# All groups but two of an MLP's down projection as seven block products, with their running sums in PSUM and the weight sums on GpSimd

## The chip, the cores and the metric

The kernel runs on one core of a Trainium2 chip. The metric is the device time of one execution in microseconds. Before the change the median of 3 runs was 2968.75 us (2968.43 to 2971.05).

## The reference

One layer of a streaming encoder on 512 tokens of width 2048, in float32: two groups of sequence mixers, cross-attention, an MLP and a last norm. The change lies in the MLP and the norm after it:

```python
hn = _rmsnorm(h, norm_mlp)                                # h: 512 x 2048
h  = h + jnp.square(jax.nn.relu(hn @ mlp_w_up)) @ mlp_w_down    # 2048 -> 8192 -> 2048
return _rmsnorm(h, norm_final)                            # h * rsqrt(mean(h*h) + 1e-6) * gain
```

## The kernel before

All is held transposed: channels on the 128 partitions, the 512 tokens along the free side (`HA` and `HB` are the tokens 0 to 255 and 256 to 511). The residual `h` is 16 tiles `hres[n]` of 128 x 512, which lie in pairs in eight tiles `hp`. Float32 products are made on TensorE from two parts: `split` (L127 on) casts a tile to fp32r on ScalarE (the high half, L130) and subtracts it from the tile on VectorE (the low half, L131); a product of weights and activations is then high x high, high x low and low x high. Split weights lie in the buffers `whi` and `wlo`, two of each, so the split of a product's weights begins when the product two before it is done.

**Up** (L1710 on) makes the 8192 hidden rows in 32 turns, each two rows of 128, by a scheme of seven block products instead of eight (`strassen`, L1293): the activations' and the weights' blocks are summed beforehand, seven products are made, and sums of products give the four result blocks. The weights' sums and the products' sums run on VectorE. The result, relu and square, goes to DRAM in `Ud`, one tile of 128 x 2 x 512 for each turn. The norm's factor isn't in it: the mean square of `h` is known only in the first turn (`rstd`, L1722), so `Ud` holds relu(.)^2 without the factor and its square 1 / (mean + eps) is multiplied in later: for the first eight rows in the turns 8 to 15 of up (L1726 to L1733: load, multiply, store), for the others when they are loaded for down (L1697, L1758).

**Down** (L1742 on) goes over the 8192 hidden rows in eight eighths `e`, each 8 tiles of 128 rows, and for each over four groups `g` of four result tiles `hres[4g]` to `hres[4g+3]`. Eighths 0 to 6 are the loop at L1860; the last eighth (L1929 on) is woven together with the last norm, in an order written out by hand. A group is made in one of two ways:

- full (`gemm`, L1869): for each of its four result tiles one weight block of 128 x 1024 is loaded and split, 24 matmuls of 512 columns are made, and one addition of 128 x 512 puts them into `hres[n]` (L1870).
- as a unit (`downunit`, L1780): four weight blocks a11, a12, a21, a22 are loaded (a11 and a12 into `wraw`, a21 and a22 into `wraw2`, three buffers each). VectorE makes four sums of them (L1820, `sub` at L1272), into two buffers `ws` and in place. Seven products follow, each with a split of 128 x 1024 and 24 matmuls of 256 columns into a PSUM bank of its own (tags `mm`, `mg` and `mx`, two banks each). The products' sums are made from PSUM into SBUF tiles `sl` (L1814, L1824) and into `hp` (`add`, L1810), twelve instructions.

Before the change the unit is used for groups 0 and 2 of the eighths 1 to 6, 12 groups of 28. The activations of a unit need their block differences (T1 to T4) as well: `downpair` (L1744) loads a pair of rows, multiplies them with the factor, splits them, makes four differences on VectorE and splits these. It is a generator: `aside` (L1844) hands the pairs of the next eighth to the groups, and after each product (or result tile) one step of it is issued. Before, pairs are made beside the full groups alone.

Loads of weights and of `Ud` go through SP's queue. Outside the last eighth the order on each engine follows the program text, as far as operands and buffers are ready when the program is laid out; on the chip each engine keeps its order.

## Time and profile before

| | us |
|---|---|
| median of 3 runs | 2968.75 |
| profiled execution, its span | 2967.1 |
| TensorE, busy | 2938.2 |
| VectorE, busy | 2323.9 |
| ScalarE, busy | 1520.1 |
| GpSimd, busy | 215.2 |
| up (from its second product to its last) | 624.3 |
| down: groups from the third of eighth 0 to the last eighth's start | 554.4 |
| the last eighth and the last norm | 105.9 |

In the profile PE is TensorE's matmuls, PEld its weight loads, DVE VectorE, ACT ScalarE, POOL GpSimd and SP the engine of the load queue. A row of the groups names the line, the engine, the operation, what it writes and reads (buffer numbers left out: `dr` and `dws` are weight blocks and sums of a unit, `d` its products, `dn` those of a full group, `de`, `do` a pair's rows, `dt` its differences), the shapes, the count, the busy time with the mean in ns, and the idle time before. A row of the timeline begins with the start in us and the duration in us.

### The profile page before, as it was taken

To read this page: it belongs to the slowest core of one execution; us is meant where nothing else is said; L and a number is where in the kernel's file an instruction comes from. 1 tells how busy PE (TensorE), PEld (TensorE's weight loads), DVE (VectorE), ACT (ScalarE), POOL (GpSimd) and SP (SyncE) were. 2 spreads that over 40 slices of the span, in tenths; PEclk is the share of its full clock that TensorE was granted. 3 is DMA by queue.
4 is the path that set the end of the run, shared out by engine and by line. 5 is a ranking of instruction groups with operands and counts; after the bars stand their busy time and mean duration, and the time that the engine had idled before them with its cause. 6 is when DMAs were issued, how large, how long until landed. Compare 5 with 4: busy or idle time off the path is not lost.

```text
span 2967.1 us, 51025 instructions
## 1 busy us (share of the span) xinstructions
PE 2938.2 (99%) x20106; PEld 2515.2 (85%) x20106; DVE 2323.9 (78%) x3725; ACT 1520.1 (51%) x2271; POOL 215.2 (7%) x552
## 2 busy tenths in 40 slices
PE   9999999999999999999999999999999999999998
PEld 7877887887788888889988988888888888998887
DVE  7677676676778667679748999999999688888777
ACT  6455555555556555654436555555555343343334
POOL 0212302302312000000000000000000000000000
PEclk9999999999999999999999999999999999999999
DMA  5333332333435587864323445444445334333436
GB/s 179 111 87 85 101 93 81 102 92 82 132 89 166 168 278 250 259 231 136 100 86 100 146 153 170 136 142 135 136 135 177 110 108 139 128 114 114 135 121 185
DMA packets 229312, 407.35 MB, mean 137 GB/s; under 512 B 92168, under 2 KB 115980, under 8 KB 229072
## 3 DMA queue, kind: packets, MB, share of 16 engines
q1 hardware_dynamic: 212944, 375.77, 41.0%
q10 hardware_dynamic: 16128, 28.32, 2.6%
q8 instruction: 158, 2.59, 0.4%
q14 instruction: 82, 0.67, 0.1%
HBM read 354.32 MB, written 49.69 MB: 136 GB/s over the span
## 4 chain that ended last, share of the span: by engine, by line
PE 86%; DVE 6%; DMA 4%; POOL 2%; issue 2%; ACT 1%; SPq 0%; ACTq 0%; DVEq 0%; POOLq 0%
PE up L122 21%; PE py L251 20%; PE dn L122 14%; PE op L122 5%; PE d L122 4%; PE vp L122 3%; PE at L122 3%; PE sc L122 3%; PE kp L251 3%; PE kq L251 2%; DVE wlo L131 2%; POOL sr L251 2%; DVE h L1810 1%; PE vo L122 1%; DMA wraw<-in_wqT 1%
## 5 line engine op out<-in xcount | busy, mean ns | idle before, releaser
L130 ACT CAST whi<-wraw 128x1024 fp32r<-128x1024 f32 x372 | 391.4, 1052 | 567.6 <-PE dn L122 189.9
L131 DVE TENSOR_TENSOR wlo<-wraw,whi 128x1024 fp32r<-128x1024 f32 x372 | 453.9, 1220 | 64.4 <-ACT whi L130 60.9
L122 PE MATMUL up<-cb,whi 128*128 128x512 f32 (+1 forms) x1904 | 451.4, 380 | 0.0
L251 PE MATMUL py<-xhi,whi 128*128 128x512 f32 x928 | 374.2, 403 | 6.6 <-ACT xhi L251 6.6
L122 PEld LDWEIGHTS up<-cb,whi 128*128 128x128 f32 x1904 | 330.7, 189 | 54.9 <-issue 0.2
L251 PE MATMUL py<-xlo,whi 128*128 128x512 f32 x928 | 374.2, 403 | 0.0
L251 PE MATMUL py<-xhi,wlo 128*128 128x512 f32 x928 | 373.6, 403 | 0.1
L251 ACT CAST whi<-wraw 128x1024 fp32r<-128x1024 f32 (+1 forms) x180 | 188.0, 1044 | 211.9 <-PE py L251 133.1
L251 DVE TENSOR_TENSOR wlo<-wraw,whi 128x1024 fp32r<-128x1024 f32 (+1 forms) x180 | 220.9, 1227 | 87.7 <-ACT whi L251 86.5
L122 PEld LDWEIGHTS up<-cb,wlo 128*128 128x128 f32 x1792 | 244.1, 190 | 16.4
L122 PE MATMUL up<-cb,wlo 128*128 128x256 f32 x1792 | 251.1, 282 | 0.0
L122 PE MATMUL dn<-uh,whi 128*128 128x512 f32 x640 | 244.7, 391 | 0.8 <-ACT whi L130 0.8
L122 PE MATMUL dn<-ul,whi 128*128 128x512 f32 (+1 forms) x648 | 244.7, 388 | 0.0
L122 PE MATMUL dn<-uh,wlo 128*128 128x512 f32 (+1 forms) x640 | 235.1, 367 | 0.0
L251 PEld LDWEIGHTS py<-xhi,whi 128*128 128x128 f32 x928 | 175.3, 189 | 41.6 <-ACT xhi L251 7.0
L1336 DVE TENSOR_TENSOR sl<-sl,up 128x256 f32<-128x256 f32 x464 | 182.0, 414 | 35.0 <-PE up L122 31.8
L251 PEld LDWEIGHTS py<-xlo,whi 128*128 128x128 f32 x928 | 175.2, 189 | 37.3 <-issue 3.3
L251 PEld LDWEIGHTS py<-xhi,wlo 128*128 128x128 f32 x928 | 175.2, 189 | 35.2 <-issue 1.0
L130 ACT CAST whi<-ws 128x1024 fp32r<-128x1024 f32 x120 | 126.1, 1051 | 108.7 <-PE up L122 70.4
L1972 POOL TENSOR_TENSOR h<-h,rstd 128x256 f32<-128x256 f32 x5 | 3.4, 724 | 2012.6 <-ACT rstd L1966 2012.6
L131 DVE TENSOR_TENSOR wlo<-ws,whi 128x1024 fp32r<-128x1024 f32 x120 | 146.0, 1218 | 0.5 <-ACT whi L130 0.5
L122 PEld LDWEIGHTS dn<-uh,whi 128*128 128x128 f32 x640 | 120.2, 188 | 26.5 <-ACT whi L130 1.0
(882 smaller groups left out, 6420.7 us busy)
## 6 DMA issues: line engine op xcount, KB each, us to landing
wraw<-in_w_up SPq DMA_DIRECT2D x128, 512.0 KB, 3.5
wraw<-in_w_in SPq DMA_DIRECT2D x116, 512.0 KB, 3.7
wraw<-in_w_dn SPq DMA_DIRECT2D x96, 512.0 KB, 3.5
wraw<-in_wk SPq DMA_DIRECT2D x32, 512.0 KB, 4.0
wraw<-in_wqT SPq DMA_DIRECT2D x32, 512.0 KB, 5.3
wraw<-in_wv SPq DMA_DIRECT2D x32, 512.0 KB, 4.8
wraw<-in_wo SPq DMA_DIRECT2D x32, 512.0 KB, 5.6
wraw<-in_w_out SPq DMA_DIRECT2D x32, 512.0 KB, 3.4
```

What stands on the lines that cost most here:

```text
L122: PE.matmul(o, l, r, start=start, stop=stop)
L130: S.copy(hi, src)
L131: V.tensor_tensor(out=lo, in0=src, in1=hi.bitcast(F32), op=ALU.subtract)
L251: f(*a, **k)
L1336: V.tensor_tensor(out=o, in0=a, in1=b, op=op)
L1810: V.tensor_tensor(out=h, in0=h, in1=two(src), op=ALU.add)
L1972: GP.tensor_tensor(out=h, in0=h, in1=rstd[:, HB], op=ALU.mult)
```

## The change

- Groups 2 and 3 of eighth 0 and all groups of the eighths 1 to 6 are units now, 26 of 28; only groups 0 and 1 of eighth 0 are full. `w_dm` holds the blocks of seven eighths and `w_dn` those of eighths 0 and 7 alone, laid out beforehand.
- A unit uses three banks, x, y and z. Products whose sum is needed go into the same bank one after the other: B11, T2, T3 and T4 into x, T1 and B22 into z, B21 alone into y. Between them VectorE adds what the bank holds so far to `hp`: seven additions of 128 x 512, the last of which (after T4) is issued in the next unit, behind its first product.
- The four weight sums of a unit run on GpSimd.
- A pair's differences run on GpSimd: two of 256 elements and one of 512 for two differences at once. A pair is loaded in one transfer (`uload`, tag `ab`, two buffers). Each group of eighths 1 to 5 prepares one pair of the next eighth, groups of eighth 0 two, those of eighth 6 a pair of the last eighth (`usplit`).
- The factor isn't multiplied into the hidden rows. `rstd` keeps mean + eps, and the residual is multiplied with it (eight products of 1024 elements in the turns 4 to 11 of up), so that `h` is divided by the square of the norm's factor. The last norm takes that back: it doesn't depend on such a scale except for its eps, which is put into the sum of squares (L1912 on).

The diff, its core:

```diff
-            if 3 < p < 8 and i == T1:
-                c = slice((p - 4) * P, (p - 3) * P)
-                V.reciprocal(out=rstd[:, c], in_=rstd[:, c])
-            if 7 < p < 16 and i in (B11, T3):
...
+            if 3 < p < 12 and i == T1:
+                h = hp[p - 4]
+                V.tensor_tensor(out=h, in0=h, in1=rstd.unsqueeze(1).broadcast_to([P, 2, T]), op=ALU.mult)
...
+    def uload(p):
+        cnt[0] += 1
+        ab = pu.tile([P, 1024], F32, tag="ab", name=f"ab{cnt[0]}", bufs=2)
+        nc.sync.dma_start(ab.rearrange("p (a b) -> p a b", b=T), Ud[p])
+        return ab
...
     def downpair(e, k):
+        ab = uload(4 * e + k)
...
+            t = utile(f"de{e}_{k}")
+            b[B11] = t[:, HA], t[:, HB]
+            split(ab[:, HA], *b[B11])
+        x = ab[:, HA]
+        GP.tensor_tensor(out=x, in0=ab[:, HB], in1=x, op=ALU.subtract)
         yield
...
+            oh, ol = utile(f"doh{e}_{k}"), utile(f"dol{e}_{k}")
+            split(ab[:, T:2 * T], oh, ol)
...
+        split(x, *b[T1])
+        x = ab[:, 0:T]
+        GP.tensor_tensor(out=pair2(x), in0=twice(ab[:, 3 * M:4 * M]), in1=pair2(x), op=ALU.subtract)
+        yield
+        yield
...
+        split(x, sh, sl)
+        x = ab[:, T:T + M]
+        GP.tensor_tensor(out=x, in0=x, in1=ab[:, HA], op=ALU.subtract)
+        yield
+        yield
+        split(x, *b[T4])
+        yield
...
+        def wsum(o, a, b, op=ALU.subtract):
...
+            GP.tensor_tensor(out=o, in0=a, in1=b, op=op)
+            return o
...
+        a11, a21, a22, a12 = raw(0), raw(1), raw(2), raw(3)
+        x, y, z = psb(f"dx{e}_{g}", "mx", 2), psb(f"dy{e}_{g}", "mg", 2), psb(f"dz{e}_{g}", "mm", 2)
+        s1 = wsum(None, a21, a22, ALU.add)
+        product(B11, a11, x, True)
+        s2 = wsum(None, s1, a11)
+        if held:
+            held.pop()()
+        product(B21, a12, y, True)
+        wsum(a21, a11, a21)
+        add(0, HA, x)
+        product(T2, s2, x)
+        wsum(a12, a12, s2)
+        add(0, HA, y)
+        product(T1, s1, z, True)
+        add(0, HB, x)
+        product(T3, a21, x)
+        add(1, HB, z)
+        product(B22, a12, z)
+        add(1, HB, x)
+        product(T4, a22, x)
+        add(0, HB, z)
+        held.append(lambda: add(1, HA, x))
...
-            if e and g % 2 == 0:
+            if e or g > 1:
                 downunit(e, g, beside)
```

## The prediction

> **What bounds the kernel now.** I read the page first: the busy shares, then the row of GpSimd in the 40 slices.

> ```profile
> PE 2938.2 (99%) x20106; PEld 2515.2 (85%) x20106; DVE 2323.9 (78%) x3725; ACT 1520.1 (51%) x2271; POOL 215.2 (7%) x552
> POOL 0212302302312000000000000000000000000000
> ```

> TensorE is busy 99% of the span, and GpSimd does nothing in the last two thirds, where the change puts its sums. A share of 99% says that fewer matmul columns are worth time, as long as the other engines keep up. So I cut the span into stretches: up, the 26 groups that the change touches (from the third group of eighth 0 to the start of the last eighth), one full group and one unit of them, and the last eighth.

> ```profile
> 1639.00:2263.29 624.29, 624.26 (x3668) 553.11 (x3668) 585.27 (x846) 339.37 (x521) 0.00 (x0) 1.00 0.44 146
> 2306.83:2861.22 554.39, 550.11 (x3361) 494.99 (x3360) 447.39 (x635) 208.08 (x289) 0.00 (x0) 1.00 0.36 118
> 2328.59:2350.35 21.76, 21.76 (x97) 18.02 (x96) 12.98 (x17) 7.25 (x10) 0.00 (x0) 1.00 0.29 97
> 2392.89:2413.67 20.78, 20.44 (x170) 20.24 (x169) 19.46 (x29) 10.20 (x15) 0.00 (x0) 1.00 0.28 89
> 2861.22:2967.10 105.88, 94.09 (x535) 80.71 (x533) 84.05 (x152) 52.31 (x77) 3.45 (x5) 0.96 0.58 179
> ```

> Columns: stretch, its length, then busy us (and count) of PE, PEld, DVE, ACT, POOL, the granted clock, DMA. A full group takes 21.76 us, a unit 20.78. The full group leaves VectorE a third free; in the unit VectorE is busy 19.46 of 20.78. The next rows show what a unit's products cost on TensorE, and what its last one loses.

> ```profile
> 2395.76 0.28 PE L122 MATMUL d<-uh,whi 128*128 128x256 f32 x1
> ...
> 2398.64 0.28 PE L122 MATMUL d<-dt,whi 128*128 128x256 f32 x1
> ...
> 2410.93 0.39 PE L122 MATMUL d<-dt,wlo 128*128 128x256 f32 x1 [0.34 <-DVE wlo L131]
> ```

> Two products begin 2.88 us apart, so seven need 7 x 2.88 = 20.16 us of TensorE; the rest of the 20.78 is a wait for VectorE's low half of the last weights. TensorE sets the pace, with VectorE close behind it in units.

> **The change on TensorE.** Of the 26 groups, 12 were units and 14 were full. All become units. With nothing in the way the stretch would take 26 x 20.16 = 524.2 us instead of 554.39: **30.2 us less**. That is all that can be won here.

> **What the other engines must do in a unit.** The first of a unit's four weight sums and its additions before, all on VectorE (12 units):

> ```profile
> L1820 DVE TENSOR_TENSOR dws<-dr,dr 128x1024 f32<-128x1024 f32 x12 | 14.6, 1219 | 0.9 <-DMA dr<-in_w_dm 0.9
> ...
> L1810 DVE TENSOR_TENSOR h<-h,d 128x512 f32<-128x512 f32 x72 | 48.0, 679 | 1.6 <-PE d L122 0.8
> ...
> L1810 DVE TENSOR_TENSOR h<-h,sl 128x512 f32<-128x512 f32 x36 | 23.6, 683 | 0.1
> ...
> L1814 DVE TENSOR_TENSOR sl<-sl,d 128x512 f32<-128x512 f32 x24 | 16.4, 683 | 2.3 <-PE d L122 2.3
> ```

> There were four sums of 1024 elements and 6 + 3 + 2 = 11 additions of 512. After: no sum on VectorE and 7 additions, since PSUM keeps the running sums. The price in PSUM is a wait: T2 may enter the bank of B11 only when B11's addition has read it; another product (2.88 us) lies between and the addition takes 0.68, so it costs nothing as long as VectorE isn't late. The seven low halves stay. A unit now has one pair of activations to prepare beside it in each group (before, in the full groups): three low halves of 256 elements and two of 512. Their spacing when VectorE has no gap:

> ```profile
> 2506.69 1.22 DVE L131 TENSOR_TENSOR wlo<-wraw,whi 128x1024 fp32r<-128x1024 f32 x1
> 2507.82 1.22 DVE L1272 TENSOR_TENSOR dr<-wraw,dr 128x1024 f32<-128x1024 f32 x1
> 2508.96 1.29 DVE L1758 TENSOR_TENSOR de<-de,rstd 128x512 f32<-128x512 f32 x2
> ...
> 2487.48 0.42 DVE L1272 TENSOR_TENSOR de<-do,de 128x256 f32<-128x256 f32 x1
> 2487.82 0.68 DVE L1810 TENSOR_TENSOR h<-h,sl 128x512 f32<-128x512 f32 x1
> 2488.42 1.22 DVE L131 TENSOR_TENSOR wlo<-dr,whi 128x1024 fp32r<-128x1024 f32 x1
> ```

> 1.137 us for 1024, 0.60 for 512, 0.34 for 256. So VectorE's own work in a unit is 7 x 1.137 + 7 x 0.60 + (2 x 0.60 + 3 x 0.34) = 7.96 + 4.20 + 2.22 = 14.4 us of 20.16. By itself that fits. ScalarE (10.20 us in a unit now) loses a copy and gains casts for the pair; it fits too. Loads don't grow: a group had four weight blocks of 512 KB as a full group and has four as a unit, and a pair comes in one DMA instead of two. GpSimd's queue holds nothing else here.

> **What the sums cost on GpSimd.** No row shows a sum of 1024 elements there; these are the nearest, with the VectorE instructions that ran at the same time.

> ```profile
> L1972 POOL TENSOR_TENSOR h<-h,rstd 128x256 f32<-128x256 f32 x5 | 3.4, 724 | 2012.6 <-ACT rstd L1966 2012.6
> ...
> 230.94 1.23 DVE L251 TENSOR_TENSOR wlo<-wraw,whi 128x1024 fp32r<-128x1024 f32 x1 [0.21 <-ACT whi L251]
> 231.51 1.81 POOL L251 TENSOR_TENSOR gEs<-gE,cst 128x512 f32<-128x512 f32 x1 [1.49 <-ACT gE L251]
> ...
> 673.81 1.29 POOL L251 TENSOR_TENSOR gEs<-gE,cst 128x512 f32<-128x512 f32 x1
> 674.12 2.06 DVE L251 TENSOR_TENSOR wlo<-wraw,whi 128x1024 fp32r<-128x1024 f32 x1 [0.17 <-ACT whi L251]
> ...
> 453.61 1.29 POOL L251 TENSOR_TENSOR gEs<-gE,cst 128x512 f32<-128x512 f32 x1
> 453.89 1.56 DVE L251 TENSOR_TENSOR gkn<-gk,sg 128x512 f32<-128x512 f32 x1 [0.72 <-ACT sg L251]
> ```

> And the end of the kernel, where VectorE's third input comes from PSUM and GpSimd runs the row above:

> ```profile
> 2957.64 4.01 DVE L1974 SCALAR_TENSOR_TENSOR h<-h,prm,row 128x256 f32<-128x256 f32 x10 [1.31 <-ACT rstd L1966]
> ```

> The same GpSimd product of 512 elements takes 1.29 us, and 1.81 when a low half had begun before it: it ends 233.32 - 232.17 = 1.15 us after the low half. The other way round, a low half that takes 1.23 takes 2.06 when a GpSimd product had begun: it ends 676.18 - 675.10 = 1.08 us after it. A 512 product on VectorE takes 1.56 instead of the 0.68 above, and ends 0.55 after. So while one of the two engines works on two SBUF tensors, the other waits until it is done. The last row is the exception: VectorE reads `row` from PSUM there, GpSimd runs its five `h<-h,rstd` in the same 4 us, and ten instructions in 4.01 us, 0.40 each, leave no room for a wait.

> [...]

> GpSimd's time grows by 1.29 - 0.724 = 0.57 us for 256 elements, so it holds the other off for 1.15 us with 512, about 0.58 with 256 and 1.15 + 2 x 0.57 = 2.29 with 1024 (an estimate from these rows). A unit has four sums of 1024, and its pair has two differences of 256 and one of 512: 4 x 2.29 + 2 x 0.58 + 1.15 = **11.5 us**. VectorE's own such work is 7 x 1.08 + 2 x 0.55 + 3 x 0.28 = **9.5 us** (the last by halving 0.55). Together 21.0 us in which one of the two must stand still or do something else: more than the 20.16 that TensorE needs.

> **The unit's time, from both sides.** Below: all of VectorE's 4.20 us of additions and all its waits for a cast fall where GpSimd works, and the unit takes 21.0 us. Above: each GpSimd instruction is waited out in full by a low half, and the unit takes 14.4 + 11.5 = 25.9 us. Between: additions are 4.20 of VectorE's 14.4 us, so by chance 29% of GpSimd's time falls beside one; 14.4 + 0.71 x 11.5 = 22.5 us. But VectorE can't be busy all the time:

> ```profile
> L130 ACT CAST whi<-ws 128x1024 fp32r<-128x1024 f32 x120 | 126.1, 1051 | 108.7 <-PE up L122 70.4
> ```

> That is the cast, 1.05 us; and what it waits for in the groups, in us, times and the longest:

> ```profile
> ACT whi L130 <- PE d L122: 103.1, 71, 2.4
> ```

> A cast waits until a product gives its buffer back, and the low half comes 1.05 us later. TensorE needs it two matmuls (0.24 us) into the product after next, which allows 2.88 + 0.24 - 1.05 - 1.22 = 0.85 us of delay, while a sum holds it 2.29. Behind it stand the additions for which the banks wait. Three sums also come in a row, since three buffers hold the second and third weight blocks of two units, so that the next unit's third block, which the first sum needs, is loaded only when T3's split has freed one. I take the middle of 22.5 and 25.9: **24.2 us**, that is 4.0 more than TensorE needs.

> The two units of eighth 0 have two pairs beside them: VectorE 16.6, GpSimd 13.8; from 16.6 + 0.75 x 13.8 = 26.9 to 30.4, middle 28.6 us. The four of eighth 6 have only four low halves of 256: VectorE 13.5, GpSimd 9.2; 13.5 + 0.69 x 9.2 = 19.8, so TensorE's 20.16, to 22.7; middle 21.4 us.

> Sum: 20 x 24.2 + 2 x 28.6 + 4 x 21.4 = 626.8 us, against 554.4: **72.4 us more**. Ends: 20 x 22.5 + 2 x 26.9 + 4 x 20.16 = 584.4 (+30) and 20 x 25.9 + 2 x 30.4 + 4 x 22.7 = 669.6 (+115).

> **The rest.** In up, TensorE is busy 624.26 of 624.29 us and VectorE 585.27. Eight products with the factor (1024 elements, 1.14 us each, 9.1 in all) come, and eight of 512 (0.60 each), the reciprocals and sixteen DMAs on SP's and ScalarE's queues go: some 4 us more in 39 that are free. I take nothing; its end is 4 us, if none of it finds a gap. In the last turn of up six splits instead of three follow T1: nothing, at most 3 x 0.60 = 1.8 us. In the last eighth each half gains one addition and one scaled square of 256 (about 0.8 us) on VectorE, busy 84.05 of 105.88: nothing, at most 1.6. The multiplications of the activations by the factor (0.60 each) go from the groups; that is in the sums above, since 14.4 us is without them.

> **The number.** The profiled execution spans 2967.1 us; the median of the runs is 2968.75, 1.65 above it. 2967.1 + 72.4 + 1.65 = **3041 us**, 2.4% slower.

> **Rivals.**
> Faster (chance 0.07): the sums don't hold up the low halves, so the place is the pair of engines in each unit, and the price is the 30.2 us: 2938.5 us. It decides at 554.4 / 26 = 21.3 us per unit: as long as a unit loses less than 21.3 - 20.16 = 1.1 us to GpSimd's work, the change wins. For it: the largest GpSimd instruction that the trace shows has 512 elements, in another stage. Against it: the stretched instruction is the very `wlo<-wraw,whi` that a unit makes seven times, and it was stretched by all that was left of GpSimd's work.
> No change (0.05): the order of work happens to put additions and casts beside GpSimd so well that only the 21.0 us count: 20 x 21.0 + 2 x 25.2 + 4 x 20.16 = 551.0, 3 us less, 2965 us. Against it: GpSimd's instructions wait for loads and for each other, not for VectorE's free time.
> Worse than forecast (a part of slower): each sum is waited out, 3083 us.

> **How the numbers follow.** Slower holds 0.88: 0.62 around 3041 with ends 2999 and 3070, 0.20 near full waiting up to 3085, 0.03 between no change and 2990, 0.03 beyond 3085. The range 2990 to 3085 leaves out the faster case, no change and these two edges, 0.18. A measurement of this kernel can tell about 0.2% (6 us) from no change; both rivals of 2938 and 2965 lie on their sides of it.

> **What would show it.** In the profile after, `wlo<-` rows of the 26 groups should have a mean well above 1.22 us (each unit's 11.5 us over 12 low halves would add up to 0.9), TensorE's idle time should be put down to DVE wlo, and units should be 22 to 26 us long; the seven additions should stay at 0.68. GpSimd's sums should read 2.4 us alone and up to 3.5 behind a low half. If the low halves stay at 1.22 and units take 20.2, the step on shared waiting is wrong; if they are long but TensorE doesn't wait, the step on the 0.85 us of slack is. Up and the last eighth should keep 624 and 106 us within 4.

## The result, and the profile after

The changed kernel takes 3103.75 us (median of 4 runs, 3100.72 to 3104.74) against 2968.59 for the kernel before beside it (2968.26 to 2971.05): a ratio of 1.0452, with a 95% interval of 1.0437 to 1.0467. It is slower, as forecast, and by nearly twice as much: 135 us instead of 72, outside the range.

The page after, its busy shares and two rows of the 40 slices:

```profile
PE 2972.7 (96%) x21114; PEld 2579.1 (83%) x21114; DVE 2454.9 (79%) x3549; ACT 1552.7 (50%) x2289; POOL 612.6 (20%) x740
...
PE   9999999999999999999999999999997887888898
...
POOL 0211311321221000000000000000046555555420
```

TensorE has lost its solid row of nines exactly in the slices where GpSimd has become half busy. TensorE's busy time has not fallen, though it has fewer columns to compute: it grew from 2938.2 to 2972.7.

The trace after cut at the same places as before: up, the first two groups of eighth 0 (still full), the 26 units, the last eighth, and then four successive units, those of one eighth. Columns as before: length, then busy us and count of PE, PEld, DVE, ACT and POOL, granted clock, DMA share, GB/s.

```profile
1639.00:2263.86 624.86, 624.82 (x3671) 553.58 (x3671) 585.64 (x839) 339.23 (x520) 3.08 (x2) 1.00 0.44 140
2263.86:2319.33 55.47, 48.37 (x194) 37.80 (x193) 42.03 (x47) 22.25 (x43) 31.20 (x26) 0.94 0.47 149
2319.33:2996.64 677.31, 579.24 (x4369) 557.02 (x4368) 570.15 (x483) 238.51 (x300) 365.18 (x161) 0.94 0.31 98
2996.64:3102.90 106.26, 94.83 (x536) 81.00 (x534) 85.48 (x156) 52.19 (x77) 3.45 (x5) 0.95 0.63 183
...
2473.84:2511.56 37.72, 26.81 (x168) 25.56 (x169) 33.92 (x32) 12.59 (x20) 26.58 (x15) 0.77 0.36 113
2511.56:2532.74 21.18, 20.58 (x170) 20.26 (x169) 16.35 (x14) 7.34 (x7) 8.62 (x4) 1.00 0.28 95
2532.74:2555.47 22.73, 21.17 (x171) 20.36 (x169) 19.21 (x15) 7.33 (x7) 11.42 (x5) 1.00 0.30 93
2555.47:2580.90 25.43, 21.32 (x170) 20.34 (x168) 21.23 (x18) 10.37 (x14) 14.45 (x7) 1.00 0.29 87
```

Of the 135.8 us by which the profiled span grew (2967.1 to 3102.9), up has 0.6, the first two groups 11.9 (43.54 before, from the ends of the stretches shown there: 2306.83 - 2263.29), the 26 units 122.9 (554.39 before) and the last eighth 0.4. The four units are very unlike: the first of an eighth takes 37.7 us and has 32 VectorE instructions and 15 of GpSimd in it, the second takes 21.2 with 14 and 4. And the granted clock, 1.00 in this stretch before, is 0.94 in the mean and 0.77 in the long unit.

Who TensorE waited for, over the whole execution after (us in total, times, the longest):

```profile
PE dx L122 <- DVE wlo L131: 62.1, 66, 3.5
PE dx L122 <- DVE h L1810: 18.7, 13, 2.6
PE dx L122 <- ACT whi L130: 10.9, 5, 2.2
```

The groups of instructions behind it, in the window of the groups (count | busy us, mean ns | idle before):

```profile
L131 DVE TENSOR_TENSOR wlo<-wraw,whi 128x1024 fp32r<-128x1024 f32 x80 | 153.3, 1916 | 8.7 <-ACT whi L130 8.5
L131 DVE TENSOR_TENSOR wlo<-dr,whi 128x1024 fp32r<-128x1024 f32 x51 | 94.6, 1855 | 13.6 <-ACT whi L130 13.6
L131 DVE TENSOR_TENSOR wlo<-dws,whi 128x1024 fp32r<-128x1024 f32 x52 | 87.6, 1686 | 5.3 <-ACT whi L130 4.9
...
L1810 DVE TENSOR_TENSOR h<-h,dx 128x512 f32<-128x512 f32 x102 | 69.5, 681 | 47.6 <-PE dx L122 47.6
```

The low halves, which read two SBUF tensors, went from 1.22 us to 1.7 to 1.9; the additions, whose second input is in PSUM, stay at 681 ns. Here is how it looks in time (start, duration), GpSimd first, then VectorE, in the trace after:

```profile
2526.45 2.42 POOL L1792 TENSOR_TENSOR dws<-dr,dr 128x1024 f32<-128x1024 f32 x1 [9.96 <-DMA dr<-in_w_dm]
2528.95 3.27 POOL L1792 TENSOR_TENSOR dws<-dws,wraw 128x1024 f32<-128x1024 f32 x1
2532.17 3.38 POOL L1792 TENSOR_TENSOR dr<-wraw,dr 128x1024 f32<-128x1024 f32 x1
```

```profile
2524.45 1.22 DVE L131 TENSOR_TENSOR wlo<-wraw,whi 128x1024 fp32r<-128x1024 f32 x1 [0.32 <-ACT whi L130]
2526.33 0.69 DVE L1810 TENSOR_TENSOR h<-h,dx 128x512 f32<-128x512 f32 x1 [0.65 <-PE dx L122]
2527.29 2.66 DVE L131 TENSOR_TENSOR wlo<-dr,whi 128x1024 fp32r<-128x1024 f32 x1 [0.27 <-ACT whi L130]
2529.87 0.67 DVE L1810 TENSOR_TENSOR h<-h,dz 128x512 f32<-128x512 f32 x1
2530.47 2.82 DVE L131 TENSOR_TENSOR wlo<-wraw,whi 128x1024 fp32r<-128x1024 f32 x1
```

The first sum finds VectorE in an addition from PSUM and takes 2.42 us. The low half that starts 0.84 us into it ends at 2529.95, 1.08 us after the sum. The second sum starts inside that low half and ends at 2532.22, 2.27 us after it. So the two take turns, and 2.42 alone and up to 3.38 behind a low half are what the prediction named.

There is a second kind of wait in the 26 units. ScalarE casts a pair's differences, and before it can, it waits for GpSimd to make them, 115.8 us in all (`dth` and `dsh` behind `ab`, up to 4.6 us at a time); the casts of weights that come later in ScalarE's order stand behind these waits.

Last, TensorE after, at the start of the long unit:

```profile
2473.84 0.76 PE L122 MATMUL dx<-de,whi 128*128 128x256 f32 x2 [2.18 <-ACT whi L130]
2477.83 0.58 PE L122 MATMUL dx<-de,wlo 128*128 128x256 f32 x1 [3.24 <-DVE wlo L131]
2478.21 0.64 PE L122 MATMUL dx<-de,whi 128*128 128x256 f32 x2
2478.64 0.41 PE L122 MATMUL dx<-de,wlo 128*128 128x256 f32 x1
```

After waits of 2.18 and 3.24 us two matmuls of 256 columns take 0.43 us from start to start instead of 0.24: the clock has been halved, from 2473.9 to 2480.7. From the starts of the matmuls and the trace's records of the clock, I divide the 677.3 us of the 26 units: 524.2 are TensorE's work at full clock, 116.6 are waits (gaps between starts beyond what a matmul needs, so they come out above the idle times of the rows above, which end with a modelled end), 26.8 are what matmuls at half clock took longer (81.9 us ran at half clock), and 10.4 are small restarts after waits (the matmul at 2530.01, at full clock after 0.60 us of waiting, takes 0.22 us to the next start instead of 0.12). These parts overshoot the stretch by 0.7. Before, the same stretch was 7.8 us longer than its matmuls need (12 x 20.16 + 14 x 21.76 = 546.6 of 554.4), all of it at full clock.

### The profile page after: what moved, and what is told of

Its sections match the earlier page's. It is cut to its first block, busy times and chain, and to the rows that moved or that the text cites. A ratio compares the mean times of both kernels' runs of the same rounds, so it can differ in the third digit from the quotient of the medians.

```text
span 3102.9 us, 53230 instructions
## 1 busy us (share of the span) xinstructions
PE 2972.7 (96%) x21114; PEld 2579.1 (83%) x21114; DVE 2454.9 (79%) x3549; ACT 1552.7 (50%) x2289; POOL 612.6 (20%) x740
## 4 chain that ended last, share of the span: by engine, by line
PE 77%; DVE 10%; issue 4%; POOL 3%; DMA 3%; ACT 3%; ACTq 0%; SPq 0%; DVEq 0%; POOLq 0%
PE up L122 20%; PE py L251 19%; PE dx L122 6%; DVE wlo L131 5%; PE op L122 5%; PE dn L122 3%; PE kq L251 3%; PE vp L122 3%; PE at L122 3%; PE sc L122 3%; PE kp L251 2%; PE dz L122 2%; ACT whi L130 2%; POOL sr L251 1%; DVE h L1810 1%
## 5 line engine op out<-in xcount | busy, mean ns | idle before, releaser
L130 ACT CAST whi<-wraw 128x1024 fp32r<-128x1024 f32 x358 | 376.0, 1050 | 491.2 <-PE up L122 178.2
L131 DVE TENSOR_TENSOR wlo<-wraw,whi 128x1024 fp32r<-128x1024 f32 x358 | 494.6, 1382 | 66.9 <-ACT whi L130 63.4
L122 PE MATMUL up<-cb,whi 128*128 128x512 f32 (+1 forms) x1904 | 451.3, 380 | 0.0
L251 PE MATMUL py<-xhi,whi 128*128 128x512 f32 x928 | 374.1, 403 | 6.5 <-ACT xhi L251 6.5
L122 PEld LDWEIGHTS up<-cb,whi 128*128 128x128 f32 x1904 | 330.7, 189 | 54.8 <-DVE cb L1269 0.2
L251 PE MATMUL py<-xlo,whi 128*128 128x512 f32 x928 | 374.3, 403 | 0.0
L251 PE MATMUL py<-xhi,wlo 128*128 128x512 f32 x928 | 373.5, 402 | 0.1
L1792 POOL TENSOR_TENSOR dws<-dr,dr 128x1024 f32<-128x1024 f32 x26 | 69.7, 2682 | 1469.2 <-DMA dr<-in_w_dm 1456.4
L251 ACT CAST whi<-wraw 128x1024 fp32r<-128x1024 f32 (+1 forms) x180 | 188.0, 1044 | 213.7 <-PE py L251 133.3
L251 DVE TENSOR_TENSOR wlo<-wraw,whi 128x1024 fp32r<-128x1024 f32 (+1 forms) x180 | 222.1, 1234 | 88.8 <-ACT whi L251 87.6
L122 PEld LDWEIGHTS up<-cb,wlo 128*128 128x128 f32 x1792 | 244.1, 190 | 16.5 <-DVE wlo L131 0.2
L122 PE MATMUL up<-cb,wlo 128*128 128x256 f32 x1792 | 251.2, 282 | 0.0
L251 PEld LDWEIGHTS py<-xhi,whi 128*128 128x128 f32 x928 | 175.3, 189 | 41.2 <-ACT xhi L251 6.5
L251 PEld LDWEIGHTS py<-xlo,whi 128*128 128x128 f32 x928 | 175.3, 189 | 36.8 <-issue 3.3
L251 PEld LDWEIGHTS py<-xhi,wlo 128*128 128x128 f32 x928 | 175.4, 189 | 35.3 <-issue 1.0
L130 ACT CAST whi<-ws 128x1024 fp32r<-128x1024 f32 x120 | 126.2, 1052 | 110.7 <-PE up L122 73.1
L131 DVE TENSOR_TENSOR wlo<-ws,whi 128x1024 fp32r<-128x1024 f32 x120 | 146.2, 1219 | 1.4 <-ACT whi L130 1.1
L122 PE MATMUL dx<-dsh,wlo 128*128 128x256 f32 x416 | 123.6, 297 | 18.9 <-DVE wlo L131 18.9
L122 PE MATMUL dx<-dsh,whi 128*128 128x256 f32 x416 | 121.2, 291 | 5.6 <-DVE h L1810 5.6
L122 PE MATMUL dx<-dsl,whi 128*128 128x256 f32 x416 | 120.1, 289 | 0.0
```

Source lines behind the costliest of these rows:

```text
L122: PE.matmul(o, l, r, start=start, stop=stop, skip_group_check=again)
L130: S.copy(hi, src)
L131: V.tensor_tensor(out=lo, in0=src, in1=hi.bitcast(F32), op=ALU.subtract)
L251: f(*a, **k)
L1792: GP.tensor_tensor(out=o, in0=a, in1=b, op=op)
```

## The experiments

My theory after the result: VectorE's and GpSimd's instructions that read two SBUF tensors exclude each other (the prediction's step); what the forecast lacked is the clock, which halves behind the waits, and the uneven order of the units. Rivals: the running sums in PSUM make the unit slow in itself; the waits are a matter of the low half's slack alone; or the loss comes from waiting for GpSimd's results, not from what it reads.

**e1: the four weight sums on VectorE, as they were in the units before; the pairs' differences stay on GpSimd.** Line 1792 of the kernel after:

```diff
-            GP.tensor_tensor(out=o, in0=a, in1=b, op=op)
+            V.tensor_tensor(out=o, in0=a, in1=b, op=op)
```

> The changed kernel with the four weight sums of a unit on VectorE again; the pairs' differences stay on GpSimd. Shared access (the low halves wait while GpSimd reads SBUF): VectorE's own work in a unit is 14.4 + 4 x 1.14 = 18.9 us of TensorE's 20.16, GpSimd's only 2.3, so units of 20.2 to 21.5 us, low halves near 1.22 us, about 2960 us in all. The rival, that the unit itself is slow (products wait for the additions that read their bank): the sums' engine doesn't matter, 3050 us or more.

Measured: 2991.19 us, ratio 1.0076 (1.0061 to 1.0091). The expected size was missed by some 31 us: 112 of the 135 us are gone, but the kernel doesn't become faster than before. What is left is with the differences, as the next one shows.

**e2: e1, and the three differences of a pair on VectorE too** (`GP` to `V` at lines 1753, 1766 and 1773), so that GpSimd does nothing beside the units.

> The changed kernel with the weight sums and the pairs' differences on VectorE; GpSimd does nothing in down. Shared access: no low half is stretched; VectorE's own work in a unit is 18.9 + 1.3 = 20.2 us, as much as TensorE's 20.16, so units of 20.2 to 21 us and 2940 to 2965 us. The rival that the unit itself is slow: 3050 us or more.

Measured: 2951.76 us, ratio 0.9947 (0.9932 to 0.9962): faster than before by 17 us. The 26 units of e2:

```profile
2306.30:2843.84 537.54, 533.13 (x4370) 526.13 (x4368) 520.01 (x657) 241.49 (x308) 0.00 (x0) 1.00 0.39 124
```

The same seven products and the same running sums in PSUM, with VectorE 520 of 537.5 us busy, and TensorE keeps its pace: 537.54 / 26 = 20.7 us a unit, at clock 1.00. So the rival that the unit itself is slow has fallen. From e2 to e1, three small differences per pair on GpSimd cost 39 us, 8.5 of them in the first two groups (52.0 against 43.55).

These 39 us are not shown to be the shared access alone. In the 26 units of e1 VectorE is busy 515.0 of 569.9 us, less than in e2, and the low halves of the weights take 1.22 to 1.30 us. What has grown most is ScalarE's waiting for a difference: 56.8 us in e1's units for GpSimd's, 6.9 in e2's for VectorE's. The round trip from ScalarE to GpSimd and back is a rival here that no run separates from the access.

**e3: the differences on VectorE, the sums on GpSimd**, the other half alone:

> The changed kernel with the pairs' differences on VectorE; the four weight sums stay on GpSimd. Shared access: GpSimd still holds VectorE off for 9.2 us in a unit, VectorE's own work is 15.7 us, so units of 22.5 to 25 us, 3020 to 3070 us: the four sums carry most of the loss. If the loss came from GpSimd's differences standing between VectorE's splits (each difference is a round trip between the two engines): about 2990 us.

Measured: 3068.07 us, 1.0340 (1.0323 to 1.0357). The sums alone cost 116 us against e2, the differences alone 39; together 155 where the change pays 152 against e2. The two nearly add up. The size is as expected, and the other reading in the expectation, that the differences carry most of the loss (about 2990 us), has fallen.

**e4: the order of the text.** The kernel after lets the program lay out VectorE's and ScalarE's order; here the loop over the groups keeps them as written:

```diff
+    spread_ = tc.manual_schedule(engines={nc.vector.engine, nc.scalar.engine})
+    spread_.__enter__()
     for e in range(7):
...
     held.pop()()
+    spread_.__exit__(None, None, None)
```

> The changed kernel with VectorE's and ScalarE's order in the groups kept as the program text has it, so that each unit prepares one pair instead of three or four pairs in the first unit of an eighth. If the bunching costs time: units of 24 to 25 us all alike instead of 37, 21, 23 and 26, hardly any time at half clock, 3040 to 3065 us. If it only moves the waits about: 3090 to 3110 us.

Measured: 3101.61 us, 1.0451 (1.0434 to 1.0469). Missed in sum and in the clock, nearly right in the units. Each unit of eighths 1 to 5 now takes 24.2 to 26.1 us (the two of eighth 0 take 29.9 and 28.7), and the 26 together 658.6, 18.7 less than after; but the first two full groups take 72.0 instead of 55.5, since in the order of the text a residual's addition stands ahead of the next block's split, and TensorE waits for the low half. The waits of e4:

```profile
PE dx L122 <- DVE wlo L131: 79.9, 61, 3.6
PE dn L122 <- DVE wlo L131: 17.3, 8, 3.8
```

and its units as one stretch, then two units one after the other:

```profile
2333.80:2992.38 658.58, 568.74 (x4369) 554.43 (x4368) 558.33 (x503) 242.84 (x318) 360.20 (x173) 0.95 0.33 104
...
2568.46:2592.86 24.40, 20.93 (x170) 20.32 (x169) 22.11 (x20) 9.29 (x12) 14.55 (x8) 1.00 0.34 108
2592.86:2618.17 25.31, 22.16 (x170) 21.75 (x169) 20.70 (x20) 9.29 (x12) 13.65 (x8) 0.93 0.34 105
```

In the units 102.3 us are waits, 26.4 slower matmuls (64.8 us at half clock, 81.9 in the kernel after, where hardly any was expected to be left), 6.3 restarts. Of the twenty units of eighths 1 to 5, the seven at full clock take 24.2 to 24.4 us, the thirteen with a window at half clock 25.0 to 26.1. The waiting now sits in one place, once per unit: three sums in a row, and the first product of the next unit behind them. GpSimd and VectorE of e4, and TensorE there:

```profile
2487.26 2.40 POOL L1792 TENSOR_TENSOR dws<-dr,dr 128x1024 f32<-128x1024 f32 x1 [5.77 <-DMA dr<-in_w_dm]
2489.74 3.27 POOL L1792 TENSOR_TENSOR dws<-dws,wraw 128x1024 f32<-128x1024 f32 x1
2492.97 2.55 POOL L1792 TENSOR_TENSOR dr<-wraw,dr 128x1024 f32<-128x1024 f32 x1
```

```profile
2488.32 2.43 DVE L131 TENSOR_TENSOR wlo<-dr,whi 128x1024 fp32r<-128x1024 f32 x1 [0.28 <-ACT whi L130]
2490.67 2.62 DVE L131 TENSOR_TENSOR dtl<-ab,dth 128x256 fp32r<-128x256 f32 x1
...
2493.81 2.79 DVE L131 TENSOR_TENSOR wlo<-wraw,whi 128x1024 fp32r<-128x1024 f32 x1
```

```profile
2496.66 0.39 PE L122 MATMUL dx<-de,wlo 128*128 128x256 f32 x1 [2.73 <-DVE wlo L131]
```

A `dtl` of 256 elements, 0.42 us in the mean of e2, takes 2.62 here: what an instruction loses goes by what the other engine has under way, not by its own size. The low half that the new unit needs ends at 2496.60, and the matmul that uses it starts 0.06 us later.

**e5: the kernel before, with the sums of its 12 units on GpSimd** (lines 1820 to 1832, `V` and `sub` to `GP.tensor_tensor`):

> The kernel before with nothing changed but the four weight sums of its 12 units on GpSimd. Shared access: VectorE's own work in such a unit falls from 20 to about 15 us, but GpSimd holds it off for up to 9.2, so units of 21 to 24 us instead of 20.8, 2975 to 3010 us. If what is slow is the changed kernel's chain of products in one bank: the sums leave VectorE, units of 20.2 us, 2961 us.

Measured: 2984.30 us, 1.0060 (1.0045 to 1.0075), as expected. In the old unit too, with eleven additions, moving the sums to GpSimd costs, 17.3 us against the kernel before beside it (2966.99), or 1.4 us a unit. That it costs less there, because the full groups between the units leave VectorE room, is my reading; no run tests it.

**e6: after, with the low-half matmuls at the end of each product.** The order of the 24 matmuls only: the 16 that read the high half first, then the 8 that read the low half.

```diff
+            for q, k in order_:
+                o, wh, wl, bh, bl = at(q, k)
+                mm(o, wh, bh, start=first and q + k == 0, stop=False, again=True)
+                mm(o, wh, bl, start=False, stop=False, again=True)
+            for q, k in order_:
+                o, wh, wl, bh, bl = at(q, k)
+                mm(o, wl, bh, start=False, stop=q == 1 and k == 3, again=True)
```

> The changed kernel with the order of a unit's matmuls changed: the 16 with the high weights first, the 8 with the low ones last. TensorE needs the low half 1.92 us into a product instead of 0.24, so a delay of 2.5 us is free instead of 0.85. Shared access: TensorE's waits for low halves (about 70 us) fall to a third, the low halves stay as long as they are, 3020 to 3050 us. The rival that products wait for additions in their banks: no gain, 3090 us or more.

Measured: 3056.13 us, 1.0294 (1.0278 to 1.0309), 48 us less than after and just above what was expected. The waits of e6:

```profile
PE dx L122 <- DVE wlo L131: 29.4, 18, 3.9
PE dx L122 <- DVE h L1813: 22.8, 9, 3.0
```

The low half is needed 14 matmuls (1.7 us) later, and the waits for it fall from 62 to 29 us; but the 19 us at the additions for which the banks wait don't fall, they are 23 now. More slack helps, but VectorE's lateness isn't a matter of one slack alone.

**e7: e2 with work on GpSimd that nobody uses**, in one kernel four subtractions of 1024 elements per unit, which read SBUF, in the other ten fills of 1024, which only write it. Both compute the full result beside it. In both a copy of one element of each partition comes first, so that the work starts behind the last addition of the unit before. The one with reads:

```diff
+    def beside_(h):
+        GP.tensor_copy(out=junk[:, 0:1], in_=h[:, 0, 0:1])
+        for _ in range(4):
+            GP.tensor_tensor(out=junk, in0=junk, in1=junk, op=ALU.subtract)
```

and the other has `for _ in range(10): GP.memset(junk, 0.0)`.

> The kernel with all sums and differences on VectorE (2952 us), and in each unit four GpSimd instructions beside it that subtract a scratch tile of 1024 elements from itself: they read SBUF for as long as the four weight sums would, and no other engine uses or waits for their result. They begin when the last addition of the unit before is done. Shared access: low halves are stretched as in the changed kernel and, since VectorE has no time to spare, units take 24 to 28 us, 3040 to 3150 us. If the loss came from waiting for the sums' results: 2952 us.

> The same, but the GpSimd instructions are ten fills of the scratch tile in each unit (about 9 us), which write SBUF and read none. If the access that the two engines share is that of reading: 2952 us, low halves of 1.22 us. If any work of GpSimd on SBUF holds VectorE off: as with reads, 3040 us or more.

Measured: reads 3127.95 us, 1.0540 (1.0525 to 1.0556); writes 2952.00, 0.9945 (0.9930 to 0.9960), the same as e2's 2951.76. GpSimd's and VectorE's groups in the kernel with reads, then in the one with writes (both from 2310 to 2950 us):

```profile
L1786 POOL TENSOR_TENSOR junk<-junk 128x1024 f32<-128x1024 f32 x89 | 226.8, 2549 | 7.0
L131 DVE TENSOR_TENSOR wlo<-dws,whi 128x1024 fp32r<-128x1024 f32 x46 | 88.0, 1913 | 1.1 <-ACT whi L130 1.1
```

```profile
L1786 POOL MEMSET junk<- 128x1024 f32 x250 | 238.9, 955 | 14.4
L131 DVE TENSOR_TENSOR wlo<-dws,whi 128x1024 fp32r<-128x1024 f32 x52 | 63.5, 1221 | 1.4 <-ACT whi L130 1.4
```

This is the verdict on the shared access. About as much GpSimd time, and no result that the unit waits for: the reads cost 176 us, the writes nothing. Beside the fills, which only write SBUF, the low halves of `dws` keep 1.221 us; beside the subtractions, which read it, they take 1.913.

**e8: e2 with e6's order**, the version that the experiments so far pointed to:

> All sums and differences on VectorE and the eight matmuls with low weights last in each product. With all on VectorE the groups still wait 13 us (537.5 instead of 524.2 us); the later need for the low half should take most of that: 2940 to 2945 us. If VectorE's 20.2 us of work are the bound, not the lateness of single low halves: 2950 us.

Measured: 2946.03 us, 0.9917 (0.9904 to 0.9931), just above the expected span and the fastest of all: 22.8 us under the kernel before, with units of 20.2 to 20.6 us, one of 21.2, against TensorE's 20.16. Together the 26 take 531.8.

**e9: e8 with one of the four sums on GpSimd.** If slack were the only limit, e8's would now be 0.85 + 1.7 = 2.5 us, more than the 2.29 of a sum.

```diff
-        wsum(a12, a12, s2)
+        GP.tensor_tensor(out=a12, in0=a12, in1=s2, op=ALU.subtract)
```

> The same as the kernel with all on VectorE and low weights last, but one of the four sums (the last, a12 - s2) on GpSimd. VectorE's own work falls from 20.2 to 19.1 us in a unit, GpSimd holds it off once for up to 2.3 us, which the 2.5 us of slack can hide. If the slack hides it: 2936 to 2942 us, no worse than all on VectorE. If VectorE has too little time left to catch up after each hold: 2950 to 2975 us.

Measured: 2968.39 us, 0.9996 (0.9987 to 1.0005): one sum in four takes all of e8's gain. The units of e8 and of e9:

```profile
2306.80:2838.60 531.80, 528.26 (x4369) 524.99 (x4368) 514.84 (x655) 240.51 (x308) 0.00 (x0) 1.00 0.39 124
```

```profile
2310.60:2863.63 553.03, 533.24 (x4370) 526.96 (x4368) 529.90 (x630) 241.88 (x308) 73.49 (x26) 1.00 0.39 120
```

```profile
PE dx L122 <- DVE h L1813: 19.5, 30, 1.3
```

VectorE has one sum less in each unit (630 instructions in the stretch instead of 655) and is busy 15 us longer, the clock stays at 1.00, and TensorE waits for VectorE's additions, not for low halves. So slack alone doesn't decide: VectorE was busy 97% of e8's stretch, and the sum took more of its time than it spared.

**e10: e4's order from the third group on only**, so that the first two full groups keep the laid-out order:

> The changed kernel with VectorE's and ScalarE's order as in the text from the first unit on; the two full groups before it stay as the program lays them out. Text order from the first group on took 18.7 us from the 26 units and gave 16.5 back in the two full groups. If both are what the spread of the pairs does: about 55 us for the two groups and 655 to 660 for the units, 3080 to 3090 us. If the early pairs only move their waits: 3100 us.

Measured: 3103.05 us, 1.0443 (1.0427 to 1.0459). This did not separate what it should: in its trace the two full groups take 72.0 us again, with their instructions in e4's order, and the units 660.9. It repeats e4 and adds nothing to it.

**e11: e4 with the clock kept up.** Twenty spare matmuls of 256 columns (2.4 us), into a bank of their own, stand in each unit's first product ahead of the matmul that waits for the low half. The result is computed in full beside them.

```diff
+                    if i == B11 and q + k == 0:
+                        spare = psb(f"keep{e}_{g}", "scr", 1)
+                        for _ in range(20):
+                            mm(spare[:, 0:M], hi[:, sl], bh, again=True)
                     mm(o, lo[:, sl], bh, start=False, stop=q == 1 and k == 3, again=True)
```

> The kernel in text order (3101.6 us; each unit waits 3 to 4 us for the low half of its first product, and the granted clock falls to half for 3.4 us in many of these waits) with 20 matmuls of 256 columns into a spare bank put in front of that wait: 2.4 us of TensorE's time in each of 26 units (62 us in all) that nobody needs. If the half clock costs what its longer matmul spacing says (26 us in the units): the added matmuls fill time that was idle, the clock stays at 1.0 in most units, and the kernel is faster than without them by 10 to 25 us, 3077 to 3092 us. If the clock's fall costs nothing of its own: 3100 us when the wait covers them, up to 3164 us when it doesn't.

Measured: 3091.09 us, 1.0410 (1.0392 to 1.0427), that is 10.5 us less than e4 with 62.4 us of unneeded matmuls more. Its units, and the spare matmuls in one of them:

```profile
2333.20:2982.60 649.40, 609.70 (x4890) 593.30 (x4889) 581.59 (x503) 242.84 (x318) 368.92 (x173) 0.99 0.34 105
```

```profile
2491.07 2.56 PE L122 MATMUL keep<-de,whi 128*128 128x256 f32 x20
2493.98 0.39 PE L122 MATMUL dx<-de,wlo 128*128 128x256 f32 x1 [0.35 <-DVE wlo L131]
```

Half clock in the units falls from 64.8 to 6.8 us, the loss by slow matmuls from 26.4 to 2.3, the waits from 102.3 to 52.6, since the spare matmuls fill them. So the half clock comes from TensorE standing still, and it is a cost of its own on top of the waits; the units of e4 with and without it (25.0 to 26.1 us, 24.2 to 24.4) say the same. The gain in the units, 658.6 - 649.4 = 9.2 us, is smaller than the 24.1 us of slow matmuls that are gone. For the most part it isn't that the spare matmuls outlast the wait, since in 19 of the 26 units TensorE still waits for the low half behind them; waits and spare matmuls together are 115.0 us, 12.7 more than e4's waits. A TensorE at half clock may give VectorE time to catch up; that isn't shown.

## Why the prediction was right in direction and wrong in size

**The ideal, 30.2 us less, stands.** e8 takes 531.8 us for the 26 units and so wins 22.6 of the 30.2, with the sums where they don't hurt. The rival "faster" was right about what the products can give and wrong about this change.

**The shared access stands, and its prices.** Sums of 2.4 us alone and up to 3.4 behind a low half, low halves lengthened by what is left of the sum, additions from PSUM at 681 ns: each as the prediction worked it out, and e7 shows that subtractions on GpSimd whose result nobody uses do this by themselves (low halves of `dws` of 1.913 us, 1.221 beside fills).

**The waiting, taken at the middle of two bounds, was right for the common unit; that the total fits is luck in part.** The forecast's 626.8 us are 102.6 over the 524.2. e4, in which every unit has its pair beside it as the prediction assumed, has 102.3 us of waits there, and its units of eighths 1 to 5 at full clock take 24.2 to 24.4 us, against the forecast's 24.2. But the middle was a guess between two balances of busy time. In e4 the wait sits behind three sums in a row, and it hardly depends on what else the unit has beside it: the units of eighth 6, put at 21.4 us for their lighter work, take 23.8 to 25.4.

**The step that failed is the sum "20 x 24.2 + 2 x 28.6 + 4 x 21.4 = 626.8", which came out at 677.3.** It took a late low half as a wait only, with matmuls of 2.88 us a product before and after it. Three things lie beside that:

- The clock, a term that the sum doesn't have. The waits come up to 3.5 us at a time, and matmuls behind them run at half clock. In the units after, that is 26.8 us of slower matmuls. The prediction read a granted clock of 1.00 before and took it along. e11 shows that the half clock hangs on the standing still. Another 10.4 us are restarts, which aren't shown to be the clock's: e11, nearly all at full clock, still has 7.9 us of them (649.4 - 524.2 - 62.4 - 52.6 - 2.3). Together they are 37.2 of the missing 50.5.
- "One pair of activations to prepare beside it in each group". The trace after doesn't have it: an eighth's first unit has 15 GpSimd instructions beside it, the second only its own four sums. The bunched units lose 37.7 - 20.16 = 17.6 us, and the empty ones don't win it back, since nothing is faster than 20.16. The units' waits are 116.6 against the forecast's 102.6: 14.0 us, which with the 37.2 are the 50.5 and the 0.7 of overshoot. What the bunching costs by itself stays open: e4 has 18.7 us less in the units but 16.5 more in the two full groups, and e10 didn't separate the two. The upper bound of 25.9 us a unit, thought a bound for waiting, is exceeded by the mean of all 26, 677.3 / 26 = 26.05.
- Outside the sum, the first two groups, which are still full, were taken as unchanged; their pairs' differences went to GpSimd as well, and they lose 11.9 us. e1 puts 8.5 of it on the differences (52.0 against e2's 43.55).

Of the error, 135.8 - 72.4 = 63.4 us, the units have 50.5, these groups 11.9, up and the last eighth 1.0.

**Up, the last eighth, ScalarE's work and the waits in PSUM at nothing:** right within 1 us for the first two; e2 shows for the others that the unit runs at 20.7 us. ScalarE's waits for GpSimd's differences, 115.8 us in the units after, are in no term of the sum; how much of them reaches TensorE isn't shown.

**The 0.85 us of slack** was told as a place where lateness gets through. e6 and e9 correct it: with more slack the waits at the additions remain (23 us in e6) or are nearly all that is left (19.5 in e9). My reading is that what counts with the sums is how full VectorE is, 520 of 537 us in e2, so that time which GpSimd takes from it is late in the end. In e9 26 sums left VectorE and its low halves of sums grew from 1.21 to a mean of 2.04 us; the busy time went up by 15.1 us and the stretch by 21.2. Where the other 6 us of that are, these runs don't settle; nor was a layout tried in which the order is laid out and the pairs are still spread.

## What to carry to other kernels

When work moves to GpSimd, don't count its time there; count what its sums of SBUF tensors take from VectorE's instructions that read two SBUF tensors (here low halves of 1.22 us became 1.7 to 1.9), per stage, and compare that with the time VectorE has free: here an engine that stood idle had nothing to give. GpSimd's fills, which only write (low halves of 1.221 us beside them), and VectorE's additions with an input in PSUM (681 ns) were exempt. Look also at which engine waits for GpSimd's result, and what stands behind that wait in its order. And where TensorE is the bound, price a wait above its length: the half clock behind the waits cost 26.8 us on 116.6 here, and a mean over units hides the long waits that bring it.

## What the runs showed of the hardware that was not expected

```profile
2470.48:2473.90 3.42, 1.24 (x11) 1.00 0.18 73
2473.90:2477.31 3.41, 0.69 (x2) 0.50 0.48 154
2477.31:2480.73 3.42, 2.90 (x13) 0.50 0.47 141
2480.73:2484.14 3.41, 3.41 (x31) 1.00 0.03 12
```

A window with 1.24 us of work is followed by one at half clock, one with 0.69 by another, one with 2.90 by full clock. I cut seven of the traces (after, e1, e3, e4, e6, the reading e7, e11) along this grid from the groups to the end. 111 windows at full clock were followed by half clock: all but one of them had under 2.0 us of work (the one, 2.12, lies in the last 20 us of a kernel), and every window under 1.5 us was among them. Between 1.5 and 2.0 both occur. So a wait of 2 us can cost a window at half clock where it falls inside one: the wait of 2.18 us in the trace after, up to 2473.84, lies in the first of the four windows. And it can cost none where a border of the grid divides it: the wait of 2.73 us in e4 shown above leaves 2.31 and 1.79 us of work in its two windows, and the next is at full clock.

The differences in the pairs cost more than their size says. In e1 the differences of 20 pairs fall in the 26 units. By the prediction's estimate they hold VectorE off for 2.3 us a pair and spare it 1.3 us of its own work (0.60 + 2 x 0.34), 20 us net, where VectorE had 537.5 - 520.0 = 17.5 us free in e2. By this the units would lose some 3 us (an estimate), yet they lose 32.4 (569.9 in e1 against 537.5 in e2), and VectorE is busy less than in e2. So VectorE's time alone doesn't explain it; ScalarE's waits for the differences are the nearest sign of where the rest lies.
